# Nine weight buffers for eight, three buffers of transposed rows for four, and another order of the experts

## The chip, the cores and the metric

One core of one Trainium2 chip runs the whole kernel in one launch. The metric is the device time of the launch in microseconds (us), lower is better; three runs of the kernel before took 1425.23 to 1426.45 us, their median is 1425.55 us.

## What is computed

The reference is one encoder block on 1536 tokens of 1024 features (a trunk of 1024 and one of 512), in float32. A mixer (pooling and differential attention) gives `h`; the part that matters here follows it:

```python
ff = hier_moe(rmsnorm(h), ...)     # router: 2 of 32 experts for each token, with gates
# per expert e, on the rows (tokens) that chose it:
hid = silu(xblk @ w_gate[e]) * (xblk @ w_up[e])    # 1024 -> 512
y   = hid @ w_down[e]                              # 512 -> 1024
out = rmsnorm(h + segment_sum(y * gate))
```

Every expert has three matrices of 2 MB, whatever its number of rows.

## The kernel before

The mixer and the router fill the first half of the time; what the change touches is the loop over the experts (`experts`, from line 1289), which TensorE (PE) runs from about 697 to 1373 us. A closing part of some 50 us follows (`close`, line 1223).

**Slots.** The loop goes over 32 slots. Slots 0 and 1 are experts 0 and 1. The other 30 experts are ranked by their number of rows at run time, and `ORDER` (line 49) says which rank comes in slots 2 to 31. Each rank has a fixed capacity, `CAPS` (line 50): ranks 0 to 7 hold 252 to 160 rows, ranks 8 to 16 hold 128 to 72, ranks 17 to 29 hold 64 or fewer. In this document an expert of ranks 0 to 7 is *heavy* (H), of ranks 8 to 16 *medium* (M), of ranks 17 to 29 *light* (L). A heavy has two blocks of rows (at most 128 each), the others have one. A light is `whole`: its product takes the float32 weights straight out of the buffer in which they landed. For a heavy or a medium each weight is first split in two parts, high and low (`split`, line 1050: ScalarE copies the high part, `split_hi`, line 103; VectorE subtracts to get the low part, `split_lo`, line 107), and each product is three matmuls (two for a block of 64 rows or fewer).

**The stream of weights.** A load is 1 MB, half of one matrix; it is used in two pieces, so a matrix is two loads and four pieces. The order of the stream (lines 1334 to 1339), of PE's products and of the pieces is the same: for each slot `i` the gate matrix of `i`, the up matrix of `i`, then the down matrix of `i - 1`. The loads are issued on SyncE's queue (`fetch`, line 1042, issue on line 1047) into `RAW` = 8 buffers of 8 KB per partition; a load waits until the one eight before it has been given up: by VectorE, after the split, for heavy and medium, and by PE, after the product, for a light. The split parts have `CUT` = 8 buffers, one piece each.

**The order on the engines.** `tc.manual_schedule` (line 1420) keeps PE, VectorE (DVE), ScalarE (ACT) and SyncE in the order in which the program issues. After each piece that PE uses, `use` (line 1404) ticks and then issues the split of the piece that lies `AHEAD` = 7 further:

```python
fn(bl, ps, pieces.pop(parts[at[2]]), h)
at[2] += 1
tick()
split(at[2] + AHEAD)
```

Everything else is hung on the ticks by `DELAY` (line 48): the activation of the gate product (`silu`, line 1174) and the product with up (`hidden`, line 1179) one tick after theirs, the output of the down product (`out`, line 1183; ACT on lines 1194 or 1198) one tick after it, the transposes of the hidden rows of slot `i - 1` in the gate of slot `i`, and `turn_x` (line 1152), the transposes of the gathered rows of slot `i + 1`, from the last piece of the up matrix of slot `i` on, one step after each piece of the down matrix of slot `i - 1`. A step is `fill` (PE transposes, line 1129, into one of two PSUM banks) and, one tick later, `empty` (ACT line 1138 and DVE line 1139 copy the bank, high and low part; line 1134 for a light). A heavy of two blocks of over 64 rows has four such steps, one with a second block of 64 or fewer three, a medium two, a light one. With two banks the third `fill` has to wait for the first `empty`. That `empty` stands in ACT's and DVE's order behind the splits issued up to its tick. The transposed rows go to tiles with the tag `x` of 8 KB per partition, four buffers (line 1156).

Gathers (line 1149) and the scatter-add of the outputs (line 1204) are indirect DMAs on GpSimd's (POOL's) queue.

Of the kernel before, what the change touches and what calls it, by code (L numbers as in the profile page):

```python
# [30 lines left out]
ES = NT + 128  # L31
TROWS = NE * ES
STATIC = 2
RAW, CUT = 8, 8
AHEAD = 7
SOON = 6
FIRST = 2
# [8 lines left out]
PACE = (3, 1, 1, 1, 1, 1, 1, 0)  # L46
WHOLE = 64
DELAY = dict(out=1, hidden=1, silu=1, evac=1, turn_h=2, turn_x=4, end_h=3, stack=3)
ORDER = (0, 17, 18, 13, 1, 19, 20, 14, 2, 21, 22, 8, 3, 23, 24, 15, 4, 27, 9, 5, 26, 16, 6, 25, 10, 12, 7, 11, 29, 28)
CAPS = (252, 252, 208, 200, 192, 160, 160, 160, 128, 112, 108, 100, 96, 88, 80, 76, 72, 64, 64, 60, 60, 56, 56, 52, 48, 36) + (32,) * 4 + (148, 48)  # L50
VORDER = tuple(range(8, 12)) + tuple(range(8))
TGORDER = (2, 0, 1)
# [1038 lines left out]
class Block:  # L1091
# [60 lines left out]
    def turn_x(self, pool=None):  # L1152
        if self.early:
            self.x = self.E.rows().bitcast(F32R).rearrange("p (o k m) -> p o k m", o=1, k=8)
        else:
            self.x = self.columns("x", 8, 4)
        return self.turn(self.x, self.xg, 8, pool)

    def turn_h(self):
# [58 lines left out]
def slots():  # L1218

    return [(NE - STATIC + e, e) for e in range(STATIC)] + [(j, None) for j in ORDER]  # L1220

# [362 lines left out]
```

## Time and profile before

| | |
|---|---|
| median of three runs | 1425.55 us |
| the profiled execution, its own time | 1428.79 us |
| its span, first to last instruction | 1426.9 us |
| PE busy | 1312.8 us (92% of the span) |
| VectorE, ScalarE, GpSimd busy | 810.1, 658.3, 235.0 us |
| mean granted TensorE clock | 0.963 |
| moved by DMA | 335.06 MB, of it 302.95 MB on SyncE's and ScalarE's queues |
| median time from issue to landing of a weight load | 14.2 us (gate), 11.7 us (up), 16.3 us (down) |

Times in the profile count from the span's start. The 1.9 us between the profiled execution's time and its span lie around the program. In a timeline the bracket at the end of a row is the idle time of the engine before it and what ended it. Matmuls overlap: each record lasts longer than the step from one to the next. A float32 matmul of a light stands in the records as two.

### The profile page before, as it was taken

To read this page: it belongs to the slowest core of one execution; us is meant where nothing else is said; L and a number is where in the kernel's file an instruction comes from. 1 tells how busy PE (TensorE), PEld (TensorE's weight loads), DVE (VectorE), ACT (ScalarE), POOL (GpSimd) and SP (SyncE) were. 2 spreads that over 40 slices of the span, in tenths; PEclk is the share of its full clock that TensorE was granted. 3 is DMA by queue.
4 is the path that set the end of the run, shared out by engine and by line. 5 is a ranking of instruction groups with operands and counts; after the bars stand their busy time and mean duration, and the time that the engine had idled before them with its cause. 6 is when DMAs were issued, how large, how long until landed. Compare 5 with 4: busy or idle time off the path is not lost.

```text
span 1426.9 us, 17476 instructions
## 1 busy us (share of the span) xinstructions
PE 1312.8 (92%) x5962; PEld 897.0 (63%) x5962; DVE 810.1 (57%) x1350; ACT 658.3 (46%) x1028; POOL 235.0 (16%) x376
## 2 busy tenths in 40 slices
PE   7999999988999999998679989999999999999980
PEld 5768888855666668776447456464655665567630
DVE  5586643066988727654734363444527566587555
ACT  6321112166887713221423453535537556577551
POOL 0000000004332210211212111121212022211233
PEclk9999999999999999999889989999999999999985
DMA  8635425436650048312488988989999998999884
GB/s 284 230 111 196 155 96 148 89 86 151 160 134 33 31 167 273 122 60 96 184 295 274 345 330 302 376 328 322 370 326 378 361 370 320 355 359 370 304 333 170
DMA packets 91621, 335.06 MB, mean 235 GB/s; under 512 B 19594, under 2 KB 27274, under 8 KB 66954
## 3 DMA queue, kind: packets, MB, share of 16 engines
q1 hardware_dynamic: 79913, 302.95, 59.0%
q0 software_dynamic: 11040, 26.78, 8.0%
q10 hardware_dynamic: 576, 4.19, 0.8%
q8 instruction: 48, 0.79, 0.2%
q14 instruction: 44, 0.35, 0.1%
HBM read 281.25 MB, written 52.62 MB: 234 GB/s over the span
## 4 chain that ended last, share of the span: by engine, by line
PE 76%; DMA 12%; DVE 5%; ACT 3%; POOL 2%; issue 1%; SPq 0%; ACTq 0%; POOLq 0%; DVEq 0%
PE pm_m L112 8%; PE pm_m L114 7%; PE pm_m L113 7%; PE pm_m L1071 6%; DMA er_raw<-w_gate 6%; PE pz_z L113 5%; PE pz_z L112 5%; PE pz_z L114 5%; PE ps_sc L393 5%; PE po_o L451 5%; PE pt_t L1129 3%; PE ph_h L113 3%; PE ph_h L114 3%; PE ph_h L112 3%; PE pm_m L1083 3%; PE pt_t L438 2%
## 5 line engine op out<-in xcount | busy, mean ns | idle before, releaser
L108 DVE TENSOR_TENSOR ew_lo<-er_raw,ew_hi 128x1024 fp32r<-128x1024 f32 x216 | 257.4, 1218 | 143.6 <-ACT ew_hi L104 143.3
L104 ACT ACTIVATE ew_hi<-er_raw 128x1024 fp32r<-128x1024 f32 x216 | 220.4, 1050 | 48.9 <-DMA er_raw<-w_gate 26.6
L112 PE MATMUL pm_m<-ew_hi,ex_x 128*128 128x512 f32 (+9 forms) x352 | 142.3, 404 | 2.3 <-ACT ex_x L1138 2.3
L114 PE MATMUL pm_m<-ew_hi,ex_x 128*128 128x512 f32 (+9 forms) x352 | 140.0, 398 | 0.5 <-DVE ex_x L1139 0.5
L113 PE MATMUL pm_m<-ew_lo,ex_x 128*128 128x512 f32 (+9 forms) x352 | 139.6, 396 | 0.0
L1204 POOL DMA_INDIRECT acc<-ex_y,ex_ix x40 | 73.6, 1839 | 345.3 <-ACT ex_y L1198 138.7
L112 PE MATMUL pz_z<-xT_hi,w_hi 128*128 128x512 f32 x288 | 115.0, 401 | 8.4 <-ACT xT_hi L153 8.4
L113 PE MATMUL pz_z<-xT_lo,w_hi 128*128 128x512 f32 x288 | 115.0, 400 | 0.0
L114 PE MATMUL pz_z<-xT_hi,w_lo 128*128 128x512 f32 x288 | 113.2, 393 | 0.0
L1071 PE MATMUL pm_m<-er_raw,ex_x 128*32 128x512 f32 (+6 forms) x448 | 103.8, 598 | 0.6 <-ACT ex_x L1134 0.6
L393 PE MATMUL ps_sc<-st_st 128*128 128x512 f32 x320 | 97.5, 445 | 7.3 <-ACT sm_e L412 5.5
L408 ACT ACTIVATE sm_e<-ps_sc,sb_m 128x1024 f32<-128x1024 f32 x64 | 70.8, 1111 | 38.7 <-PE pt_t L438 37.4
L397 DVE TENSOR_REDUCE sb_m<-ps_sc 128x1 f32<-128x1024 f32 x64 | 75.3, 1218 | 22.1 <-PE ps_sc L393 22.1
L393 PEld LDWEIGHTS ps_sc<-st_st 128*128 128x128 f32 x320 | 59.7, 194 | 42.9 <-ACT sm_e L408 12.6
L112 PEld LDWEIGHTS pm_m<-ew_hi,ex_x 128*128 128x128 f32 (+9 forms) x352 | 60.7, 172 | 35.1 <-ACT ex_x L1138 9.0
L112 PE MATMUL ph_h<-wo_woh,mx_mh 128*128 128x512 f32 x192 | 78.1, 408 | 0.0
L113 PE MATMUL ph_h<-wo_wol,mx_mh 128*128 128x512 f32 x192 | 77.7, 406 | 0.0
L114 PE MATMUL ph_h<-wo_woh,mx_ml 128*128 128x512 f32 x192 | 77.6, 404 | 0.0
L451 PE MATMUL po_o<-wT_wT,v_V 128*128 128x512 f32 x160 | 77.4, 608 | 0.0
L114 PEld LDWEIGHTS pm_m<-ew_hi,ex_x 128*128 128x128 f32 (+9 forms) x352 | 60.7, 173 | 22.4 <-DVE ex_x L1139 1.2
L113 PEld LDWEIGHTS pm_m<-ew_lo,ex_x 128*128 128x128 f32 (+9 forms) x352 | 60.7, 173 | 19.8 <-issue 0.5
L112 PE MATMUL pm_m<-ew_hi,ex_h 128*128 128x512 f32 (+10 forms) x176 | 71.2, 405 | 0.0
(289 smaller groups left out, 2380.2 us busy)
## 6 DMA issues: line engine op xcount, KB each, us to landing
er_raw<-w_gate SPq DMA_DIRECT2D x64, 1024.0 KB, 14.2
er_raw<-w_up SPq DMA_DIRECT2D x62, 1024.0 KB, 11.7
er_raw<-w_down SPq DMA_DIRECT2D x62, 1024.0 KB, 16.3
st_st<-qk SPq DMA_DIRECT2D x48, 256.0 KB, 7.0
rw_raw<-w_in SPq DMA_DIRECT2D x16, 512.0 KB, 4.8
rw_raw<-xT SPq DMA_DIRECT2D x12, 512.0 KB, 5.7
x_x<-x SPq DMA_DIRECT2D x12, 512.0 KB, 5.3
qk<-rp_h SPq DMA_DIRECT2D x24, 256.0 KB
```

Source lines behind the costliest of these rows:

```text
L104: nc.scalar.activation(hi, raw, AF.Copy)
L108: nc.vector.tensor_tensor(lo, raw, hi.bitcast(F32), OP.subtract)
L112: nc.tensor.matmul(out, lhsT=xh, rhs=wh, start=first, stop=False)
L113: nc.tensor.matmul(out, lhsT=xh, rhs=wl, start=False, stop=False)
L114: nc.tensor.matmul(out, lhsT=xl, rhs=wh, start=False, stop=last)
L393: nc.tensor.matmul(sc[:, b], lhsT=st[:, cc, 0, q0:q0 + 128], rhs=st[:, cc, i, k0:k0 + 512], start=i == 1, stop=i == 2)
L397: nc.vector.tensor_reduce(m[:, :1], sc, axis=AX.XY, op=OP.max, negate=True)
L408: nc.scalar.activation(e, sc, AF.Exp, bias=m[:, :1], accum_out=acc)
L451: nc.tensor.matmul(self.o, lhsT=V[:, self.t0 // 128 + kt, self.h * 128:(self.h + 1) * 128], rhs=self.wT[:, kt], start=kt == 0, stop=kt == ...
L1071: self.nc.tensor.matmul(p[b.at(k)], lhsT=b.x[:, i * 2 + k], rhs=w[:, k * 512:(k + 1) * 512], start=i == 0, stop=i == 3)
L1083: self.nc.tensor.matmul(banks[0][b.at(hf)], lhsT=b.h[:, i], rhs=w[:, s], start=i == 0, stop=i == 3)
L1204: self.nc.gpsimd.indirect_dma_start(out=self.E.S["acc"], out_offset=bass.IndirectOffsetOnAxis(ap=self.ix[:self.m, 0:1], axis=0), in_=self. ...
```

## The change

The weight stream gets nine buffers, and the tag `x` three. `ORDER` changes. Written by class, slots 2 to 31 before:

H L L M, H L L M, H L L M, H L L M, H L M, H L M, H L M M, H M L L

and after:

H M L, H L M L, H L M L, H L M L, H L M L, H M L, H M M L, H M L L

The heavies stand in the same order (ranks 0 to 7) in both. Before, the first heavy comes after the light slot 1, and every other heavy after a medium; after, every heavy comes after a light. `E.open_weights(ctx, RAW - FIRST, CUT, side="right")` (line 1422) follows `RAW`, and so does how far ahead `fetch` is issued (lines 1383 and 1482).

```diff
-RAW, CUT = 8, 8
+RAW, CUT = 9, 8
-ORDER = (0, 17, 18, 13, 1, 19, 20, 14, 2, 21, 22, 8, 3, 23, 24, 15, 4, 27, 9, 5, 26, 16, 6, 25, 10, 12, 7, 11, 29, 28)
+ORDER = (0, 13, 17, 1, 18, 14, 19, 2, 20, 8, 21, 3, 22, 15, 23, 4, 24, 9, 27, 5, 16, 26, 6, 12, 10, 25, 7, 11, 29, 28)
-            self.x = self.columns("x", 8, 4)
+            self.x = self.columns("x", 8, 3)
```

## Rows read from the trace of the kernel before

**Rows 1.** Windows of 20 us: busy time of the engines, PEclk, DMA share, GB/s.

```profile
800.00:820.00 20.00, 17.75 (x85) 8.26 (x84) 3.73 (x4) 8.09 (x12) 2.56 (x2) 1.00 1.02 386
...
1300.00:1320.00 20.00, 20.00 (x95) 14.42 (x95) 12.89 (x15) 12.13 (x16) 1.10 (x2) 1.00 1.02 378
```

**Rows 2.** Waits of PE from 800 to 1100 us: total, times, longest.

```profile
PE pt_t L1129 <- DVE ex_x L1139: 11.3, 5, 5.3
PE pm_m L112 <- ACT ex_x L1138: 2.3, 1, 2.3
PE pm_m L1113 <- DVE ex_x L1139: 1.9, 1, 1.9
PE pm_m L114 <- DVE ex_x L1139: 0.5, 1, 0.5
```

**Rows 3.** Chain that ended last, 800 to 850 us: start, length, what.

```profile
785.09 16.51 DMA er_raw<-w_gate
...
818.31 20.69 DMA er_raw<-w_gate
...
839.09 1.06 ACT ew_hi L104
...
842.05 1.09 PE pt_t L1129 x4
...
848.40 0.23 PE pm_m L113
```

**Rows 4.** Timeline of PE, 923.8 to 929 us.

```profile
928.13 0.80 PE L1129 MATMUL pt_t<-k_ident,ex_xg 80*128 80x80 f32 x4 [3.66 <-DVE ex_x L1139]
```

**Rows 5.** Windows cut at the changes of the granted clock, columns as in rows 1.

```profile
820.60:824.00 3.40, 2.98 (x7) 1.95 (x8) 3.37 (x6) 2.60 (x4) 1.06 (x1) 0.51 1.03 403
...
841.00:848.00 7.00, 5.95 (x17) 2.10 (x17) 5.82 (x8) 4.01 (x6) 0.00 (x0) 0.51 0.41 140
...
926.40:933.20 6.80, 5.07 (x16) 1.68 (x16) 5.62 (x8) 4.39 (x7) 0.62 (x1) 0.50 0.78 302
...
1097.40:1104.00 6.60, 6.59 (x31) 5.36 (x32) 5.47 (x6) 5.69 (x7) 3.40 (x3) 1.00 1.01 415
```

**Rows 6.** Timeline of PE, 895 to 914 us: a light's gate and up.

```profile
897.43 1.93 PE L1071 MATMUL pm_m<-er_raw,ex_x 128*60 128x512 f32 x8
...
904.99 0.50 PE L1129 MATMUL pt_t<-k_ident,exa_xg 80*128 80x80 f32 x4
905.41 1.08 PE L1083 MATMUL pm_m<-er_raw,ex_h 128*60 128x512 f32 x4
```

**Rows 7.** Timeline of ACT, 735 to 760 us.

```profile
745.14 0.63 ACT L1177 ACTIVATE ex_s<-ex_t 48x512 f32<-48x512 f32 x1 [1.69 <-DVE ex_t L1171]
745.67 3.89 ACT L104 ACTIVATE ew_hi<-er_raw 128x1024 fp32r<-128x1024 f32 x4
749.59 0.60 ACT L1138 ACTIVATE ex_x<-pt_t 128x512 fp32r<-128x512 f32 x1
```

**Rows 8.** Timeline of DVE, 735 to 760 us.

```profile
751.30 0.68 DVE L1139 TENSOR_TENSOR ex_x<-pt_t,ex_x 128x512 fp32r<-128x512 f32 x1
```

**Rows 9.** Timeline of PE, 735 to 760 us: the first heavy's four transpose steps.

```profile
745.99 0.66 PE L1129 MATMUL pt_t<-k_ident,ex_xg 128*128 128x128 f32 x4
...
748.81 0.60 PE L1129 MATMUL pt_t<-k_ident,ex_xg 128*128 128x128 f32 x4
...
752.04 0.65 PE L1129 MATMUL pt_t<-k_ident,exa_xg 124*128 124x124 f32 x4 [0.32 <-DVE ex_x L1139]
...
755.08 0.64 PE L1129 MATMUL pt_t<-k_ident,exa_xg 124*128 124x124 f32 x4
```

**Rows 10.** Timeline of ACT, 1040 to 1100 us: outputs of a heavy and of a light.

```profile
1062.20 2.77 ACT L1198 ACTIVATE ex_y<-pm_m,ex_ix 128x512 f32<-128x512 f32 x4 [8.06 <-PE pm_m L114]
...
1078.40 1.37 ACT L1194 ACTIVATE ex_y<-pm_m,ex_ix 52x512 f32<-52x512 f32 x2
```

**Rows 11.** Timeline of DVE, 1060 to 1100 us.

```profile
1069.01 0.68 DVE L1171 TENSOR_TENSOR ex_t<-ex_t,pm_m 48x512 f32<-48x512 f32 x1 [13.44 <-ACT ex_t L1170]
1071.34 3.50 DVE L108 TENSOR_TENSOR ew_lo<-er_raw,ew_hi 128x1024 fp32r<-128x1024 f32 x3 [1.64 <-ACT ew_hi L104]
```

## The prediction

> **What bounds the kernel now.** I read the page's busy shares first, then the 20 us windows of the expert stage, then PE's waits, then the chain. From 1100 us on PE has no idle time worth a row and the weights come at full DMA share beside it [rows 1]; between 800 and 1100 us it waits, 16.0 us in eight waits (11.3 + 2.3 + 1.9 + 0.5) [rows 2]. So PE bounds the expert stage and any change of its idle time goes into the total almost one for one; the closing part begins when PE's last down product ends. What PE waits for is named as a vector or scalar copy of transposed rows, but the chain shows what is behind it: the load of a gate half lands at 839.0 (818.31 + 20.69), ScalarE splits at 839.09, VectorE after it, and only then comes the copy for which PE's transpose at 842.05 waits [rows 3]. The copy stands in line behind a split whose weight is late. Each such wait has a second price: after waits of 2.3 and 0.5 us, of 5.3 us and of 3.66 us [rows 2, 4] PE runs at the lower of its two clock levels, 1.2 GHz (granted 0.5), for 3.4, 7.0 and 6.8 us, while after the wait of 1.9 us it stays at 2.4 GHz [rows 2, 5].
>
> **What the change removes.** The loads are late where two lights follow a heavy. From one second gate load (slot 4) landing at 801.6 to another (slot 6) at 839.0 lie twelve loads, so 3.12 us for each, gathers and scatters included [rows 3]. A light asks for six, 18.7 us, and keeps PE for 7.6 us of gate and up (897.43 to 904.99) [rows 6] and half as much, 3.8 us, of down: 11.4 us. Each light costs 7.3 us of lead. In the new order heavies 1 to 4 each come one light sooner (slots 5, 9, 13, 17 for 6, 10, 14, 18), which leaves 7.3 us more lead in front of each, and the ninth buffer holds one more load, 3.1 us. Together 10.4 us against a longest wait of 5.3 us: I take all the late-load waits as gone. That is 16.0 us of idle time, and of the half-clock stretches half of what PE was busy in them, (2.98 + 5.95 + 5.07) / 2 = 7.0 us [rows 5]. **Removed: 23.0 us.** The two ends for this term are zero (the lead is used up elsewhere) and 23.0.
>
> **What it costs in buffers.** Three tiles of transposed rows instead of four: I cost it at nothing. `turn_x` of slot `i + 1` is issued after the last up product of slot `i` on the same engine, so PE has finished with the old tiles before the new ones are written; at most two blocks are live, and three tiles hold a heavy and one more. If that cover were gone the price would be a medium's gate and up in front of each heavy, so it would show at once. Gathers and scatters move with their slots, equally many. On SyncE's queue the small index loads come one weight load later in the queue than now; they are issued four slots ahead, so I take zero; a late one would show as PE waiting for a gather.
>
> **What it adds.** The new order puts a light in front of heavies 1 to 7; now only the first heavy, in slot 2, has one (slot 1). That place is in the trace. The light's second activation starts on ACT at 745.14, four splits follow it, and only then the first copy of the heavy's transposes [rows 7]; VectorE's copy ends at 751.98 [rows 8], and PE's third step starts at 752.04 after a wait of 0.32 us, the fourth 3.04 us after it [rows 9]. So from the activation to the third step take 6.9 us, all of it ACT and VectorE in order, whatever the weights do. The wait was small only because the down pieces between the steps were long: 5.73 us from the first step (745.99) to the end of the second piece (751.72), the down of a 148-row expert at ten matmuls a piece.
>
> In the new order the down matrix there is a medium's: six matmuls a piece at 0.23 us [rows 3], 1.4 us. Count from the start of the light's gate. PE: 7.6 us gate and up, then step and piece twice, 2 x (0.4 + 1.4) (904.99 to 905.41 for the step) [rows 6], so it asks for the third step at **11.2 us**. ACT and VectorE: first the output of the slot before, 1.4 us if a light or a medium [rows 10], then the splits of three of the medium's down pieces, the first through ACT 1.0 us, three on VectorE 3.5 us, then a copy of the medium's hidden rows 0.6 and the light's own sum 0.7 [rows 7, 8, 11]: the activation starts at about 7.3, with 0.1 for the hand-overs, and 6.9 later, at **14.2 us**, PE gets its bank. The wait is 3.0 us. For heavies 1 and 6 the output in front is a heavy's, 2.8 instead of 1.4 us [rows 10]: 4.4 us. Sum 5 x 3.0 + 2 x 4.4 = 23.8 us.
>
> Then the clock. A wait of 3.0 lies between the 2.3 that cost 3.4 us and the 3.66 that cost 6.8 us at half clock; I take the shorter, 1.6 us lost (of 2.98 and 3.4 busy), and for 4.4 the longer, 2.8 us lost (of 5.07 to 5.95): 5 x 1.6 + 2 x 2.8 = 13.6 us. If the clock stays up, the fourth step of the three heavies that have one waits instead: 3.04 us after the third, with 1.8 us of step and piece in front, 1.2 us, 3.6 us in all. At half clock that step and piece cover it. **Added: 37.4 us** with the drop, 27.4 without.
>
> The sum is 37.4 - 23.0 = +14.4 us. It is made on the profiled execution (1428.79 us, span 1426.9), which ran 3.2 us above the median; on the median it gives 1425.55 + 14.4 = **1440 us**. No term changes the start (slots 0 to 2 are as before) or the closing part (the last two slots are as before, and its loads wait for the scatters).
>
> **The rivals.**
> *The clock holds after the new waits.* Then +27.4 - 23.0 = +4.4, 1430 us. For it: after 1.9 us it held. Against: 2.3 was enough to lose it.
> *The copies are not late, and it gets faster.* The place is the queue in front of the light's activation: if ACT and VectorE have the medium's down pieces split before the light begins, the activation starts as soon as its own gate allows, 3.8 + 0.6 + 0.7 = 5.1 us, and the bank is free at 12.0 us: 0.8 us of wait at seven places and the 1.2 us at three, 9.2 us, no clock lost. That gives -13.8, 1412 us. It decides from a start of about 5.5 us on: up to there the wait stays near 1 us. For it: ACT and VectorE are busy little over half of the stage. Against: those splits are issued in the light's own gate, behind the output of the slot before.
> *The buffers were the limit and nothing takes their place.* Then all 23.0 us come back, 1402.5 us. The evenly repeated wait in front of each heavy speaks for it, and the 0.32 us of [rows 9] for a small new wait. The Trainium skill (Perfetto Trace Analysis, Optimization Strategy) reads the same gap repeating on the engine that should be saturated as a possible lack of buffers; by that rule the ninth buffer would help and the time would be this rival's. The waits do repeat here, at each of heavies 1 to 4, but they shrink and end at 1100 us with the buffers unchanged, so it is also the order.
> *Both waits.* The lead is not kept, and late loads add to the late copies: half of the 23.0 stay, 1451 us.
> *It does nothing*, because SyncE's order does not let the ninth load start earlier and the waits only change places: 1425.5.
>
> **How the numbers follow.** Forecast 0.54; clock holds 0.14; faster 0.14; nothing in its place 0.06; both waits 0.07; nothing 0.05. A difference under 0.2%, 2.9 us, can't be told from no change here. Slower: the forecast, both waits, and most of clock holds, 0.72. Same: nothing and the rest of clock holds, 0.08. Faster: 0.20. The forecast and the rival above it reach to about 1450; downwards the range takes in the clock rival and most of the faster one only at its upper part, to 1416; left out are 0.05 above and about 0.13 below.
>
> **What would show it.** In the profile of the changed kernel: no wait of PE from 800 to 1100 us whose chain goes back to a weight load; instead seven waits of PE's transposes for VectorE's copy, 3 to 4.4 us, one in front of each heavy from the second on, also after 1100 us, each behind four splits in a row on ACT, with a dip of the granted clock after it. DMA share falling in front of the heavies, as the buffers are full. If instead these waits are under 1.5 us the step of the light's activation is wrong, and the time is under 1430. If their chain goes to loads, the ledger of lead is wrong. If PE waits for a matmul's reader of `x`, the three tiles are.

## The result, and the profile after

The changed kernel takes 1437.28 us (median of 20 runs) where the kernel before, beside it, takes 1424.43 us: ratio 1.0088, 95% interval 1.0068 to 1.0107, so 0.9% slower, some 12.5 us on the 1425.55 us shown ahead. The forecast was 14.4 us slower. The profiled execution took 1439.77 us (span 1437.5 us, mean granted clock 0.961), 11.0 us more than the profiled execution of before.

PE's waits in the changed kernel, 740 to 1400 us, those of the closing part left out (total, times, longest):

```profile
PE pt_t L1129 <- DVE ex_x L1139: 21.2, 11, 2.8
PE pt_t L1129 <- DVE ex_s L1181: 5.2, 1, 5.2
...
PE pm_m L1113 <- DVE ex_x L1139: 0.4, 1, 0.4
```

Against [rows 2]: the waits of up to 5.3 us are gone, and with them those on lines 112 and 114. Eleven shorter ones for the copy of line 1139 stand there now (the one of 0.3 us in front of heavy 0 was there before), and one that no part of the prediction had, for line 1181. Where they lie is in the timeline of PE of the changed kernel (the bracket is the idle time before the row; the first row and the last are the start of slot 1's gate and the last down products, the rows of line 1071 at 811.21 and 892.99 the starts of the lights' gates before heavies 1 and 2):

```profile
739.13 1.06 PE L1071 MATMUL pm_m<-er_raw,ex_x 128*48 128x512 f32 x4 [0.58 <-ACT ex_x L1134]
...
811.21 1.94 PE L1071 MATMUL pm_m<-er_raw,ex_x 128*64 128x512 f32 x8
...
818.84 0.65 PE L1129 MATMUL pt_t<-k_ident,ex_xg 128*128 128x128 f32 x4
819.25 0.48 PE L112 MATMUL pm_m<-ew_hi,ex_h 128*88 128x512 f32 x1
...
820.71 0.60 PE L1129 MATMUL pt_t<-k_ident,ex_xg 128*128 128x128 f32 x4
...
824.96 0.64 PE L1129 MATMUL pt_t<-k_ident,exa_xg 124*128 124x124 f32 x4 [2.28 <-DVE ex_x L1139]
...
892.99 1.89 PE L1071 MATMUL pm_m<-er_raw,ex_x 128*60 128x512 f32 x8
...
907.17 0.50 PE L1129 MATMUL pt_t<-k_ident,ex_xg 80*128 80x80 f32 x4 [2.79 <-DVE ex_x L1139]
910.21 0.49 PE L1129 MATMUL pt_t<-k_ident,ex_xg 80*128 80x80 f32 x4 [1.15 <-DVE ex_x L1139]
...
1369.57 0.60 PE L1129 MATMUL pt_t<-k_ident,ex_s 32*128 32x32 f32 x4 [5.20 <-DVE ex_s L1181]
...
1379.97 4.49 PE L1083 MATMUL pm_m<-er_raw,ex_h 128*32 128x512 f32 x20
```

The third step of each heavy from the second on waits: 2.28, 2.79, 2.79, 2.78, 2.72, 2.27 and 2.34 us, 18.0 in all, and three fourth steps and one product 3.4. These are the seven places that the prediction named. Behind them is no late load: ScalarE, whose first split of a piece has to wait for its weight, waited 32.1 us for weight loads between 800 and 1350 us in the kernel before,

```profile
ACT ew_hi L104 <- DMA er_raw<-w_gate: 26.6, 10, 4.4
ACT ew_hi L104 <- DMA er_raw<-w_up: 5.5, 5, 2.4
```

and has no such wait there in the changed kernel. What stands in front of them is in ACT's timeline of the changed kernel, first before heavy 1, then before heavy 2:

```profile
809.24 2.77 ACT L1198 ACTIVATE ex_y<-pm_m,ex_ix 128x512 f32<-128x512 f32 x4 [8.66 <-PE pm_m L114]
...
813.64 0.47 ACT L1138 ACTIVATE ex_h<-pt_t 128x352 fp32r<-128x352 f32 x1 [0.69 <-PE pt_t L1129]
...
818.07 0.63 ACT L1177 ACTIVATE ex_s<-ex_t 64x512 f32<-64x512 f32 x1 [1.45 <-DVE ex_t L1171]
...
893.26 1.38 ACT L1194 ACTIVATE ex_y<-pm_m,ex_ix 64x512 f32<-64x512 f32 x2 [3.07 <-PE pm_m L1083]
894.66 1.06 ACT L104 ACTIVATE ew_hi<-er_raw 128x1024 fp32r<-128x1024 f32 x1
895.75 0.44 ACT L1138 ACTIVATE ex_h<-pt_t 128x320 fp32r<-128x320 f32 x1
896.08 1.99 ACT L104 ACTIVATE ew_hi<-er_raw 128x1024 fp32r<-128x1024 f32 x2
...
900.27 0.63 ACT L1177 ACTIVATE ex_s<-ex_t 60x512 f32<-60x512 f32 x1 [1.57 <-DVE ex_t L1171]
900.81 3.89 ACT L104 ACTIVATE ew_hi<-er_raw 128x1024 fp32r<-128x1024 f32 x4
904.72 0.60 ACT L1138 ACTIVATE ex_x<-pt_t 128x512 fp32r<-128x512 f32 x1
```

The row 900.81 is the queue of [rows 7]: four splits between the activation and the first copy. The light's gate before heavy 2 starts at 892.99; its activation comes 7.28 us later and the third step 14.18 us later (the prediction had 7.3 and 14.2).

Windows of the changed kernel, columns as in [rows 1]: one of 20 us, then the stretches where the granted clock is down, and one (1074) behind a wait of 2.78 us where it stays up:

```profile
800.00:820.00 20.00, 20.00 (x91) 12.14 (x92) 4.97 (x7) 9.11 (x13) 4.72 (x3) 1.00 0.92 308
...
991.20:998.00 6.80, 5.99 (x18) 4.09 (x17) 5.78 (x8) 4.80 (x7) 0.76 (x1) 0.50 1.05 279
...
1074.00:1077.50 3.50, 3.45 (x20) 2.42 (x21) 3.47 (x5) 3.50 (x5) 0.00 (x0) 1.00 1.04 320
1151.60:1155.00 3.40, 3.40 (x10) 2.42 (x9) 3.40 (x5) 2.67 (x4) 0.00 (x0) 0.50 1.01 417
1216.50:1219.90 3.40, 3.40 (x10) 2.01 (x9) 3.40 (x5) 2.59 (x3) 0.00 (x0) 0.50 1.05 307
1298.40:1301.80 3.40, 3.40 (x9) 2.41 (x8) 3.40 (x5) 2.60 (x4) 0.00 (x0) 0.50 0.96 364
...
1366.70:1373.50 6.80, 3.93 (x12) 1.24 (x14) 2.28 (x3) 0.28 (x1) 0.37 (x1) 0.50 0.66 162
```

In the first 20 us PE is without idle time now, where [rows 1] had 17.75 us busy, and the DMA share is 0.92 for 1.02, which fits buffers that are full part of the time. Behind four of the seven waits the clock fell to the lower level, behind three it did not. Half of the busy time in the four stretches is (5.99 + 3 x 3.40) / 2 = 8.1 us, and by the last row 2.0 us more are lost around the wait that ends at 1369.57.

That last wait comes from an order. VectorE's mask for the closing part (line 1356) is issued with the load stream, as the step after its last loads. One buffer more brings that step one load earlier in the program, and so ahead of the light's sum and product (lines 1171 and 1181) in VectorE's order. VectorE's timeline, first of the kernel before:

```profile
1354.36 0.67 DVE L1171 TENSOR_TENSOR ex_t<-ex_t,pm_m 32x512 f32<-32x512 f32 x1
1355.06 0.68 DVE L1181 TENSOR_TENSOR ex_s<-ex_s,ex_t 32x512 f32<-32x512 f32 x1
1362.80 1.02 DVE L1356 TENSOR_SCALAR er_raw<-er_raw,ex_to 128x1536 fp32r<-128x1536 f32 x1 [7.06 <-POOL er_raw L1347]
```

and of the changed kernel:

```profile
1367.11 1.02 DVE L1356 TENSOR_SCALAR er_raw<-er_raw,ex_to 128x1536 fp32r<-128x1536 f32 x1 [8.72 <-POOL er_raw L1347]
1368.04 0.67 DVE L1171 TENSOR_TENSOR ex_t<-ex_t,pm_m 32x512 f32<-32x512 f32 x1
1368.74 0.68 DVE L1181 TENSOR_TENSOR ex_s<-ex_s,ex_t 32x512 f32<-32x512 f32 x1
```

In both, VectorE sits still some 7 to 9 us for POOL's iota (line 1347). Before, the light's work was already done; now it stands behind the wait, and PE behind it.

One gain was not foreseen either. From the first gate product of slot 1 to the last down product PE takes 1373.41 - 737.28 = 636.1 us before and 1384.46 - 739.13 = 645.3 us after. Less the idle time (16.0 of [rows 2] and 0.3 of [rows 9]; 21.2 + 5.2 + 0.4 = 26.8 now) and what the half clock cost (7.0 and 8.1 + 2.0 us), 612.8 and 608.4 us are left: PE's own work became 4.4 us shorter. The timeline of PE of the kernel before shows both ends, and between them three rows in front of heavy 3:

```profile
737.28 1.07 PE L1071 MATMUL pm_m<-er_raw,ex_x 128*48 128x512 f32 x4 [0.58 <-ACT ex_x L1134]
...
1007.09 0.60 PE L1129 MATMUL pt_t<-k_ident,ex_xg 128*128 128x128 f32 x4
1007.62 1.07 PE L1083 MATMUL pm_m<-er_raw,ex_h 128*56 128x512 f32 x4
1008.62 0.66 PE L1129 MATMUL pt_t<-k_ident,ex_xg 128*128 128x128 f32 x4
...
1369.81 3.60 PE L1083 MATMUL pm_m<-er_raw,ex_h 128*32 128x512 f32 x16
```

There the steps alternate with a light's down pieces, a step and a piece in 0.53 and 1.00 us; a light's down in one run takes 3.48 us for four pieces (889.51 to 892.99), 0.87 each. After the change they alternate with a medium's pieces, 0.41 and 1.46 us (818.84 to 820.71), where six matmuls at 0.23 us are 1.38. So a step and a piece lose less: (1.00 - 0.87) + (0.53 - 0.41) - (1.46 - 1.38) = 0.17 us, over 21 of them (four at heavies 1 to 3, three at 4 to 6; heavy 7 had a medium's pieces before, too) 3.6 us; the steps of mediums and lights are not counted. This split of the 4.4 us is an estimate from the rows. That they belong to the order shows in the profiles of the runs below: reckoned in the same way, PE's own work is 612.6 to 613.4 us in the six kernels that keep a medium in front of heavies 1 to 7, and 607.2 to 609.0 us in the five with the changed order, with eight buffers and with nine.

### The profile page after: what moved, and what is told of

Read it like the earlier page. It is cut to its first block, busy times and chain, and to the rows that moved or that the text cites. A ratio compares the mean times of both kernels' runs of the same rounds, so it can differ in the third digit from the quotient of the medians.

```text
span 1437.5 us, 17489 instructions
## 1 busy us (share of the span) xinstructions
PE 1312.1 (91%) x5962; PEld 901.5 (63%) x5962; DVE 805.3 (56%) x1350; ACT 656.5 (46%) x1028; POOL 245.3 (17%) x376
## 5 line engine op out<-in xcount | busy, mean ns | idle before, releaser
L112 PE MATMUL pm_m<-ew_hi,ex_h 128*128 128x512 f32 (+10 forms) x176 | 74.7, 425 | 0.0
```

Source lines behind the costliest of these rows:

```text
L112: nc.tensor.matmul(out, lhsT=xh, rhs=wh, start=first, stop=False)
```

## The experiments

Each diff is against the kernel named. The first four tell the two big parts and the mask apart.

**Nine buffers, old order.** Against the changed kernel:

```diff
-ORDER = (0, 13, 17, 1, 18, 14, 19, 2, ...)
+ORDER = (0, 17, 18, 13, 1, 19, 20, 14, ...)
```

> Nine weight buffers and three tiles of transposed rows, with the order of before. My theory: each late-load wait gets up to 3.1 us shorter, so of the 16.0 us between 800 and 1100 us some 2 to 6 stay; no wait of the transposes in front of heavies after mediums is added; the closing part's mask stands one load earlier in VectorE's order and holds PE near 1360 us for about 5 us plus a half-clock stretch, as in the changed kernel. Sum about -18 + 8 = -10 us, ratio to before near 0.993. Rival, the ninth buffer is worth nothing because the waits come from the order alone: 16 us of waits stay and the mask adds 8, ratio 1.005. Rival, the mask wait belongs to the new order: no wait near 1360, ratio near 0.987.

1425.54 us, ratio 0.9988 (0.9962 to 1.0015). PE's waits of this run, 740 to 1400 us, those of the closing part left out:

```profile
PE pt_t L1129 <- DVE ex_x L1139: 8.1, 4, 6.2
PE pt_t L1129 <- DVE ex_s L1181: 5.3, 1, 5.3
```

The expectation, 0.993, missed. The ninth buffer halves the waits in front of the heavies, but the longest, in front of heavy 1, stays (6.2 us); and the wait behind the mask is there with the old order too, so it belongs to the buffer and not to the order.

**New order, eight buffers.** Against the kernel before:

```diff
-ORDER = (0, 17, 18, 13, 1, 19, 20, 14, ...)
+ORDER = (0, 13, 17, 1, 18, 14, 19, 2, ...)
```

> The new order alone, with eight weight buffers and four tiles of transposed rows. My theory: the seven waits in front of heavies 1 to 7 are there as in the changed kernel, 2.3 to 2.8 us each, about 21 us with the fourth steps; no mask wait near 1360 us; the late-load waits are gone or under 5 us in all, since one light fewer stands in front of heavies 1 to 4. Ratio to before 1.003 to 1.006. Rival, the ninth buffer is what removed the late loads: they stay beside the new waits, ratio 1.012 or more, and PE waits of 4 us and more in front of the heavies.

1436.04 us, ratio 1.0059 (1.0033 to 1.0084), a ratio as expected. Two waits of PE's timeline of this run:

```profile
827.51 0.64 PE L1129 MATMUL pt_t<-k_ident,exa_xg 124*128 124x124 f32 x4 [2.28 <-DVE ex_x L1139]
...
1157.32 0.95 PE L1129 MATMUL pt_t<-k_ident,exa_xg 32*128 32x32 f32 x7 [5.97 <-DVE ex_x L1139]
```

The same seven waits come with the order alone, six of 2.3 to 3.5 us. The one of 5.97 us goes back, in the chain of waits, to a late load of a down matrix (18.5 us, landing at 1147.4): with eight buffers one late load is left in the new order. No wait stands behind the mask. Behind all seven the clock fell.

**The mask later.** Against the changed kernel:

```diff
-nc.vector.tensor_scalar(tail["hot"], tail["pos"], tail["to"], None, op0=OP.is_equal)
+after(3, lambda: nc.vector.tensor_scalar(tail["hot"], tail["pos"], tail["to"], None, op0=OP.is_equal))
```

> The changed kernel with VectorE's mask of the closing part issued three ticks later, so behind the light's hidden product as in the kernel before. My theory: PE's wait of 5.2 us near 1364 us and the 6.8 us of half clock after it go, 7 to 8 us, and the seven waits stay; ratio to before near 1.003. Rival, the mask only takes the blame and the light's hidden product is late for another reason: the wait stays, ratio 1.009.

1433.31 us, ratio 1.0032 (1.0009 to 1.0055), as expected. VectorE's timeline of this run:

```profile
1358.17 0.68 DVE L1181 TENSOR_TENSOR ex_s<-ex_s,ex_t 32x512 f32<-32x512 f32 x1
1366.17 1.02 DVE L1356 TENSOR_SCALAR er_raw<-er_raw,ex_to 128x1536 fp32r<-128x1536 f32 x1 [7.32 <-POOL er_raw L1347]
```

The product is done before the mask again, the wait of 5.2 us is gone, the seven others are as they were (17.9 us). So the mask's place was worth 1.0088 - 1.0032, 0.6% or some 8 us: 5.2 of idle time and 2.0 of half clock by the profile, and what is left over lies within the two intervals.

**Nine buffers, old order, mask later.** Both edits above, against the changed kernel:

> Nine weight buffers, three tiles, the order of before, and the mask three ticks later. My theory: what is left of the late loads, 2 to 6 us, and no other new wait: -16 to -20 us, ratio to before 0.986 to 0.989, below both kernels. Rival, lead gained by the ninth buffer is used up and the waits stay: ratio 0.998 to 1.0.

1416.68 us, ratio 0.9919 (0.9887 to 0.9950): faster than both kernels, but less so than the 0.986 to 0.989 expected. PE's waits of this run, 740 to 1400 us, those of the closing part left out:

```profile
PE pt_t L1129 <- DVE ex_x L1139: 7.7, 4, 5.3
```

The wait in front of heavy 1 is 5.3 us again, as long as before. Its load does land sooner: counted from the start of slot 1's gate, after 97.4 us (834.79 - 737.39) where the kernel before has 101.7 (839.00 - 737.28). But PE comes to its third step 4.3 us sooner as well, after 95.2 for 99.5 us (832.57 and 836.74), since the two waits ahead of it in [rows 2] (2.3 and 0.5 us) and the half clock after them are gone. What the buffer gives is used up once along the stream; it is not given again at each wait.

The four give a table, ratios to the kernel before:

| | old order | new order |
|---|---|---|
| eight buffers | 1 | 1.0059 |
| nine | 0.9988 | 1.0088 |
| nine, mask later | 0.9919 | 1.0032 |

The ninth buffer (with three tiles) is worth 0.8% in the old order when the mask is out of its way; the new order takes 0.6 to 1.1% in every row.

**Splits six pieces ahead.** What sets the seven waits? Against the changed kernel:

```diff
-AHEAD = 7
+AHEAD = 6
```

> The changed kernel with one edit: the split of a piece is issued six pieces ahead of its use instead of seven. Nothing of the computation changes. Theory (the new third-step waits come from the queue of splits in front of the light's activation): in the light's gate two of the medium's down pieces are split ahead of the activation instead of three, so activation and copy come one split, 1.15 us, sooner: the five waits of 2.7 to 2.8 us fall to about 1.6, the two of 2.3 to about 1.1, their sum from 18.0 to about 10.4 us; with up to 3 us of half clock saved the time is 1427 to 1430 us where the changed kernel takes 1437, a ratio of 1.002 to 1.0035 to the kernel before; the wait for the mask (5.2 us) stays. Rival one (the waits go back to the weights, not to this queue): they stay at 2.3 to 2.8 us and the ratio at 1.009. Rival two (the splits need the seven pieces): PE waits for split parts in new places, in the heavies' and mediums' products, and the time is not below 1437 us.

1441.00 us, ratio 1.0095 (1.0072 to 1.0117); seven waits of 2.28 to 2.51 us. The expectation missed: the 2.7 to 2.8 us fell by only 0.2 to 0.4, the 2.3 not at all. ACT's timeline of this run, in front of heavy 2, says why:

```profile
898.14 0.44 ACT L1138 ACTIVATE ex_h<-pt_t 128x320 fp32r<-128x320 f32 x1 [0.70 <-PE pt_t L1129]
898.60 2.01 ACT L104 ACTIVATE ew_hi<-er_raw 128x1024 fp32r<-128x1024 f32 x2
...
902.68 0.63 ACT L1177 ACTIVATE ex_s<-ex_t 60x512 f32<-60x512 f32 x1 [1.45 <-DVE ex_t L1171]
```

The split taken away stood ahead of the copy of the medium's hidden rows, and that copy now waits 0.70 us for PE's transposes. Two splits still stand between it and the activation. The waits are as long as rival one had them, but not for its reason: ACT waits for no weight load in this run between 800 and 1350 us. In the changed kernel ACT waits for the transposes, 0.69 us, in front of heavy 1 as well, where the wait was 2.28.

**Splits five pieces ahead**, with the mask later; against the run with the mask later alone:

```diff
-AHEAD = 7
+AHEAD = 5
```

> The changed kernel with the mask issued three ticks later (that pair of edits alone gave 1.0032 of the kernel before) and the splits five pieces ahead instead of seven. With six ahead the waits fell only to 2.3 to 2.5 us: the split that was taken away stood in front of ACT's copy of the medium's hidden rows, which then waited 0.70 us for PE's transposes, and two splits still stood between that copy and the activation. Theory (those two splits set the 2.3 us): with five ahead one is left, VectorE is through with it 1.2 us sooner and the activation comes 1.1 us sooner, so each of the seven waits falls to 1.1 to 1.4 us, their sum to some 9 us, and the ratio to about 0.998 if no new wait appears. Rival one (the activation is held by its own gate product, not by the splits): the waits stay at 2.3 to 2.5 us and the ratio at 1.003. Rival two (five pieces ahead are too few): PE waits for split parts in the heavies' and mediums' products, and the ratio is above 1.005.

1418.30 us, ratio 0.9953 (0.9932 to 0.9973), with 1.0032 for the run it is made from. Two waits of PE's timeline of this run:

```profile
823.92 0.64 PE L1129 MATMUL pt_t<-k_ident,exa_xg 124*128 124x124 f32 x4 [1.16 <-DVE ex_x L1139]
...
904.63 0.50 PE L1129 MATMUL pt_t<-k_ident,ex_xg 80*128 80x80 f32 x4 [1.25 <-DVE ex_x L1139]
```

The seven are 1.16, 1.25, 1.38, 1.23, 1.35, 1.24 and 1.21 us, 8.8 in all, as expected, and one of them alone (1.35, at 1141) is followed by a stretch at half clock. So the waits of the new order are set by the splits queued between the hidden rows' copy and the light's activation; the weights are in time, and with two splits fewer even the new order beats the kernel before. The gain is larger than the 0.998 expected; the clock, which falls behind one of the seven waits where it fell behind four in the run with the mask later, is the part of it that the profile shows. Against it stands a wait of 4.7 us for a gather in front of heavy 0's third step (at 752.77), with 3.4 us at half clock; no other profile here has it, and whether it comes from the edit is open.

**Three tiles of transposed rows.** Against the kernel before:

```diff
-            self.x = self.columns("x", 8, 4)
+            self.x = self.columns("x", 8, 3)
```

> The kernel before with three buffers of transposed rows instead of four and nothing else. Theory (a tile is written again only after PE is through with the old one): no new wait, ratio 1.000 within 0.002, PE's waits before the heavies as in the kernel before (16 us from 800 to 1100 us). Rival (the third tile is the limit in front of a heavy of two blocks): one more wait in front of each of eight heavies, up to a medium's gate and up each, and the time is slower by more than 0.5%.

1427.08 us, ratio 0.9989 (0.9970 to 1.0007), and no new wait. The longest wait, in front of heavy 1, was 8.0 us in its profile and the waits of the stage 16.4 us in all, where before has 16.3. No cost of the third tile shows.

**One light fewer before heavy 1**, eight buffers. Against the kernel before:

```diff
-ORDER = (0, 17, 18, 13, 1, 19, 20, 14, 2, 21, 22, 8, 3, 23, 24, 15, 4, 27, 9, 5, ...)
+ORDER = (0, 17, 13, 1, 18, 19, 14, 2, 20, 21, 8, 3, 22, 23, 15, 4, 24, 27, 9, 5, ...)
```

> The kernel before with one expert moved: the second light between heavies 0 and 1 (rank 18) goes behind heavy 1, and the lights after it each move on by one place, so that heavy 1 comes one slot sooner and every heavy still follows a medium. Eight buffers. Theory (each light takes 7.3 us of lead, a heavy gives it back): the late load in front of heavy 1 goes (5.3 us and some 2.8 us of half clock), and no late copy appears since mediums stay in front of the heavies; from heavy 2 on the count of lights is as before or one less, so the waits of 2.3 to 3.7 us elsewhere stay or shrink: ratio 0.990 to 0.996. Rival (the lead is only lost later): a wait of about the same size stands in front of heavy 2, ratio 0.999 to 1.001.

1423.68 us, ratio 0.9972 (0.9949 to 0.9994). The chain of this run that ended last, 870 to 910 us:

```profile
883.89 18.58 DMA er_raw<-w_gate
...
903.64 1.23 DVE ew_lo L108
...
905.52 0.79 PE pt_t L1129 x4
```

The wait in front of heavy 1 is gone, but one of 5.1 us stands in front of heavy 2, and one of 3.9 in front of heavy 5. The rival had the mechanism, a wait of about the same size in front of heavy 2; the ratio lies between the two forecasts. With eight buffers this order mostly moves the late load.

**The same order with nine buffers and the mask later**, three tiles of transposed rows.

Against the run with nine buffers, the old order and the mask later:

```diff
-ORDER = (0, 17, 18, 13, 1, 19, 20, 14, 2, 21, ...)
+ORDER = (0, 17, 13, 1, 18, 19, 14, 2, 20, 21, ...)
```

> The order of the run beside it (rank 18 behind heavy 1, a medium in front of each heavy), with nine weight buffers, three tiles of transposed rows, and the mask of the closing part issued three ticks later. Theory: with nine buffers, the old order and the late mask the time was 0.992 of the kernel before, with 5.3 us of wait in front of heavy 1 and 6.8 us at half clock after it; both go, and some 2 us of waits stay: 7 to 8 us less, ratio 0.985 to 0.988, faster than both kernels. Rival (the late load only moves to heavy 2): a wait of 3 to 5 us there, ratio 0.991 to 0.993.

1415.67 us, ratio 0.9926 (0.9899 to 0.9953): also faster than both kernels, but not told apart from 0.9919 with the old order. The waits are near what was expected, some 2 us; PE's from 740 to 1400 us in this run, those of the closing part left out:

```profile
PE pt_t L1129 <- DVE ex_x L1139: 3.3, 2, 3.0
```

The time is not: 4.4 us of idle time less than with the old order, but the one wait of 3.0 us, in front of heavy 5, is followed by 6.8 us at half clock (6.03 busy, 3.0 lost), as the wait of 5.3 us was there (4.75 busy, 2.4 lost). The first gathers differ too: PE waits 8.9 us for one at its start, 6.4 in the other run.

## Why the prediction was right, and where it was wrong

**Right in size by terms that make up for each other.** By the profiles, late loads removed 23.0 us as forecast; the seven waits with their followers added 21.4 of idle time (18.0 + 3.4) and 8.1 of half clock, 29.5 where 37.4 had been forecast; the wait behind the mask added 7.2 (5.2 + 2.0) where nothing had been; and PE's own work fell by 4.4, for which the prediction had no term either. The sum is 29.5 + 7.2 - 23.0 - 4.4 = +9.3 us, and the stage grew by 645.3 - 636.1 = 9.2; its start, 1.85 us later, and a closing part 0.4 us shorter make the 10.6 us of span. Of the later start 1.4 us are PE's wait for its first gather (10.3 us before, 11.7 after); in the eleven profiles that wait lies between 3.9 and 12.2 us, so no meaning is read into it. That the total came so near is in part luck: 7.9 us too much was forecast for the new waits, and 7.2 us behind the mask, for which the sum had nothing, nearly filled that gap.

**Late loads: right, but by two causes that do not add.** All of the 16.0 us of waits in [rows 2] went. The prediction gave 7.3 us of lead to the order and 3.1 to the buffer and took 10.4 as enough. The runs show that neither alone was. Nine buffers with the old order keep the wait in front of heavy 1 at its length. The new order with eight buffers did most: one late load is left, in front of heavy 5, 5.97 us where the changed kernel waits 2.72. One light moved, with eight buffers, clears heavy 1 and brings the late load to heavy 2 instead.

The Trainium skill (Perfetto Trace Analysis, Optimization Strategy) reads a gap that repeats on the engine that should be saturated as a possible lack of buffers. The runs bear it out in part for the waits of [rows 2], where nine buffers with the mask moved gave 0.9919 and halved them; the seven waits of the new order repeat as evenly and are no such lack: they come with eight buffers and with nine, and two splits fewer ahead of the activation cut them from 17.9 to 8.8 us.

**The seven waits: the place and the queue right.** Forecast 3.0 us at five places; at four of them (heavies 2 to 5) 2.72 to 2.79 were measured, at heavy 7 2.34. All seven lie below the 3 to 4.4 us that were to show it. The count from the light's gate, activation at 7.3 and bank at 14.2, holds at heavy 2 row for row; PE only asks 0.2 us later than counted.

**Heavies 1 and 6 at 4.4 us: wrong, and in the wrong direction.** The prediction had a heavy's output, 2.8 us instead of 1.4, hold ACT longer. It does take 2.77 us, but it begins at 809.24, 2.0 us before the light's gate at 811.21, while PE still works on the heavy's last down products; a light's output begins 0.27 us after the gate (893.26 against 892.99). So these two waited 2.28 and 2.27 us, and with heavy 7 (2.34, behind a medium's output) they are the short ones, the four behind a light's output the long ones, 2.72 to 2.79. The output's length was counted and its start was not.

**The clock after every wait: too much.** The prediction took a drop behind each of the seven waits, 13.6 us, from waits of 2.3 and 3.66 us that had each cost one. The profile has four, 8.1 us. The rival that the clock holds was partly right: behind three waits it did. The fourth steps wait besides, 1.0, 1.15 and 0.8 us where 1.2 had been forecast for a held clock; for heavy 3 with a dropped clock too.

**The closing part at nothing: wrong.** The prediction looked at the two last slots and at the loads, and left out that the steps of the closing part are issued by the count of loads, so a deeper buffer moves VectorE's mask too. That is the term of 0.6% that the run with the mask later takes away. The part behind the last down product did not become longer (53.5 us before, 53.0 after).

**The three tiles and the index loads at nothing: right.** The run with three tiles alone is no different from before, and no wait for a gather is in the profile between 740 and 1400 us.

## What to carry to other kernels

When a buffer is added to a stream whose position also triggers other work, list what else moves earlier in each engine's order, and ask what it waits for: here a mask that waited 7 us harmlessly came to stand one place ahead of work that PE needed. An order that hides the loads can lengthen a queue of copies: count, from the consumer back, the instructions issued between its last free input and the copy that it needs, and try fewer of them before another order. Change the parts one by one: here the ninth buffer was worth -0.8%, the order +0.6 to 1.1%, and the mask's move, which nobody had asked for, +0.6 to 0.7%.

## What was not expected of the hardware

After waits of the same length PE's clock fell to its lower level at one place or in one run and held at another. In front of heavy 1, 2.28 us kept it up in the changed kernel and lost it, for 3.4 us, with eight buffers (window 828.7 to 832.1, granted 0.50) and with the splits six ahead. Within the changed kernel 2.79 and 2.78 us (heavies 2 and 4) kept it, 2.79 and 2.27 us (heavies 3 and 6) lost it. Waits of 1.2 to 1.4 us lost it once in seven, in the run with the splits five ahead. No run here settles what decides, so a term for the clock is best given as a count of drops with both ends.

A float32 piece between two transposes takes 1.00 us where one in a run of them takes 0.87, and the steps themselves are 0.53 instead of 0.41 us beside it. In the profiles PE's own work in the stage is some 4.4 us shorter with the changed order, without any wait in the trace; that this alternation is the cause is worked out from the rows and not tested by itself.
